# Lower parts of four more weight blocks made by VectorE, and a longer lead for issuing transfers

## The chip, the cores and the metric

The kernel runs on one core of a Trainium2 chip. The metric is the device time of one execution in microseconds (us), taken as the median of several runs. The core's engines are TensorE (PE in the profile, its weight loads PEld), VectorE (DVE), ScalarE (ACT), GpSimd (POOL) and SyncE (SP). Each has its own instruction queue and works through it in order. Transfers are issued from the queues of SP, ACT and POOL.

## What is computed

The reference is a two-layer trunk over 512 tokens of width 1024. Layer A is a conformer convolution module and a squared-ReLU MLP, then one shared set of keys and values is made, and layer B is latent attention and another MLP. The change touches weights of the convolution module (31 taps, a filter per channel):

```python
def conformer_conv(h, w_pw1, b_pw1, w_dw, b_dw, ln_g, ln_b, w_pw2, b_pw2):
    u = h @ w_pw1 + b_pw1
    a, gate = jnp.split(u, 2, axis=-1)
    u = a * jax.nn.sigmoid(gate)
    u = jnp.pad(u, ((0, 0), (CONV_WIDTH - 1, 0), (0, 0)))
    u = lax.conv_general_dilated(u, w_dw[:, None, :], window_strides=(1,), padding='VALID',
                                 dimension_numbers=('NWC', 'WIO', 'NWC'),
                                 feature_group_count=D_MODEL) + b_dw
    u = jax.nn.silu(layer_norm(u, ln_g, ln_b))
    return u @ w_pw2 + b_pw2
```

## The kernel before

**Matrix products.** A product in float32 precision is made of three products in a shorter format: each operand is split into an upper part (rounded) and a lower part (what rounding left), and hi·hi, lo·hi and hi·lo are added in PSUM. A weight block (128 output columns, kept as 128 partitions of 1024 elements) comes into a buffer `raw` by a transfer of 512 KB that SP issues; from it come `wh` (upper) and `wl` (lower). A product of one block is 24 matmuls of 128x512. There are 5 buffers for `raw`, 5 for `wh` and 6 for `wl`, each reused in turn.

**Two ways to the lower part.** They stand in `weight()`, lines 722 to 772. In the first, `split` (line 789), ACT copies `raw` to `wh` in two halves and DVE subtracts, `wl = raw - wh`, in two halves. In the second, for names that `lo_by_dma` (line 88) gives, ACT writes `wl = -raw`, rounded, in two halves, then `wh` in two halves, and POOL issues a transfer that reads the 512 KB of the block from HBM once more and adds them into `wl` (`accum_op`). All 16 blocks of the first pointwise weights (pw1) and of the second (pw2) have such a name, and so have some of the first MLP. Line 754 keeps the first four blocks of pw1 on the first way: `i` counts pw1's blocks in the order of use (columns 0, 8, 1, 9, 2, 10, 3, 11 and so on, a value column and its gate column by turns).

**The convolution module.** When the two products of a channel block are there, DVE multiplies both out of PSUM with the norm's factor (`tmp<-mm,big`), ACT makes the sigmoid (`tmp<-tmp,vt`) and DVE the gated value (`big<-tmp,vt,tmp`). Three of the eight channel blocks (0, 1, 3) are convolved on DVE, 29 instructions `big<-big,vt,big` each, after two by ACT (`big<-big,vt`). The other five (2, 4, 5, 6, 7) go to PE (`taps_tensor`): the gated value is written to DRAM by one transfer on ACT's queue (`dealt<-big`, in `deal_tokens`, line 1151 on), read back in another layout by four more on the same queue (`uu<-dealt`, a quarter of the partitions each), and met by 72 matmuls of 128x128 (`mm<-uu,big`) with band matrices that SP loads (`big<-cw`, nine of 256 KB per channel block). The layer norm follows (`bc<-col,big` sums over channels on PE), then pw2.

**What sets the order.** The kernel does not call the engines directly. `Program` records every operation; `schedule` (line 500 on) places them one after another by costs that it assumes, the most urgent first, where `due` says by when each is needed; `run` repeats this 16 times and issues the operations in the order of the best plan. PE gets filler matmuls (`mm<-ident`) where the plan sees it idle. In `schedule`, line 548 holds a transfer back in the plan until it is at most `LEAD` ahead of its due time. Every instruction is issued on line 640 (`issue`), so that all rows of the profile read L640, and the tiles' names tell them apart. A transfer issued by SP or ACT signals its end on one of eight semaphores (DMAHW0 to DMAHW7 in the order's rows) that the two queues use in turn together; before a semaphore is used again, the transfer eight places earlier must have landed, and the issuing engine waits for that.

Of the kernel before, what the change touches and what calls it, by code (L numbers as in the profile page):

```python
# [87 lines left out]
def lo_by_dma(name):  # L88
    if name[0] == "ff1":
        return name[2] == 0 and name[3] < 4  # L90
    if name[0] == "ff2":
        return name[1] == 0 and name[2] == 3 and name[3] in LAST_BY_DMA
    return name[0] in ("pw1", "pw2")
# [154 lines left out]

PORT = ("tensor_tensor", "scalar_tensor_tensor")

LEAD = 16000.0

BESIDE = 3000.0

# [29 lines left out]
class Program:  # L284
# [166 lines left out]
    def schedule(self, tags):  # L451
# [71 lines left out]
        while left:  # L523
# [19 lines left out]
            while avail[e]:  # L543
# [3 lines left out]
                way = next(w for w in o.ways if w[0] == e)  # L547
                if way[1] == "dma_start" and o.rank > now + LEAD:

                    heappush(future[e], (o.rank - LEAD, o.n, o))  # L550
                    continue
# [92 lines left out]
def trunk(ctx: ExitStack, tc: tile.TileContext, xT, xN, wts, vec, along, rope, cw, out):  # L644
# [72 lines left out]
    def scaled(name, src):  # L717

        lo, hi = ([big(F32R) for _ in range(2)] for _ in range(2))
        for o in range(2):  # L720
            raw = big()
            nc.sync.dma_start(out=raw, in_=src[:, o * T : (o + 1) * T])
            g0 = VEC[GAINS[name[0]]] + 4 * o
            gain = vt[:, g0 : g0 + 4].rearrange("p (k o) -> p k o", o=1).to_broadcast([P, 4, P])
            nc.vector.tensor_tensor(
                out=raw.rearrange("p (k m) -> p k m", m=P), in0=raw.rearrange("p (k m) -> p k m", m=P), in1=gain, op=ALU.mult
            )
            split(raw, slice(0, T), (hi[o], lo[o]))
        return hi, lo

    def weight(key):

        while key not in blocks:
            name, parts = USE[len(blocks)]
            i, n = BLK[parts[0][0]], _cols[BLK[parts[0][0]]]
            if name[0] in GAINS:
                blocks[name] = scaled(name, wts[i])
                continue
            raw, hi, lo = nc.tile(RAW), nc.tile(WH, F32R), nc.tile(WL, F32R)
            step = 256 if i < 2 else n  # L740
            for o in range(0, n, step):
                nc.sync.dma_start(out=raw[:, o : o + step], in_=wts[i, :, o : o + step])
            for other, sign in parts[1:]:
                if sign > 0:
                    nc.gpsimd.dma_start(out=raw, in_=wts[BLK[other]], accum_op=ALU.add)
                else:
                    second = nc.tile(RAW)
                    nc.sync.dma_start(out=second, in_=wts[BLK[other]])
                    for o in range(0, n, 512):
                        nc.vector.tensor_tensor(  # L750
                            out=raw[:, o : o + 512], in0=raw[:, o : o + 512], in1=second[:, o : o + 512], op=ALU.subtract
                        )
            src = raw if len(parts) > 1 else wts[i]
            if i >= 4 and lo_by_dma(name):

                for o in range(0, n, 512):
                    for dst, scale in ((lo, -1.0), (hi, 1.0)):
                        nc.scalar.activation(dst[:, o : o + 512], raw[:, o : o + 512], AF.Copy, scale=scale)
                nc.gpsimd.dma_start(out=lo, in_=src, accum_op=ALU.add)
            else:  # L760
                step = 256 if i < 2 else min(n, 512)
                engines = VG if name[0] in ATT else ("vector",)
                for o in range(0, n, step):
                    split(raw, slice(o, o + step), (hi, lo), engines=engines)
            blocks[name] = hi, lo
        return blocks[key]
# [5 lines left out]
    def products_of(keys, X, t0, n, nk=KT):  # L772

        w = [weight(key) for key in keys]
        pts = [nc.tile(MM) for _ in keys]
        for k in range(nk):
            for (hi, lo), pt in zip(w, pts):
                ks = slice(k * P, (k + 1) * P)
                if isinstance(hi, list):
                    hi, lo, ks = hi[k // 4], lo[k // 4], slice(k % 4 * P, (k % 4 + 1) * P)  # L780

                for j, (a, b) in enumerate(((hi, X[k][0]), (lo, X[k][0]), (hi, X[k][1]))):
                    nc.tensor.matmul(
                        pt[:, :n], lhsT=a[:, ks], rhs=b[:, t0 : t0 + n],
                        start=(k == 0 and j == 0), stop=(k == nk - 1 and j == 2),
                    )
        return pts

    def split(src, s, dst, d=None, engines=("vector",)):

        d = s if d is None else d
        nc.scalar.activation(dst[0][:, d], src[:, s], AF.Copy)
        nc.binary(engines, out=dst[1][:, d], in0=src[:, s], in1=dst[0][:, d].bitcast(F32), op=ALU.subtract)
# [84 lines left out]
    def by_tokens(name, X, first=None):  # L878


        def group(dh, bs, outer):
            pts = {b: nc.tile(MM) for b in bs}
            w = [weight(name + (dh, ku)) for ku in range(4)]
            for ku, b in [(ku, b) for ku in range(4) for b in bs] if not outer else [(ku, b) for b in bs for ku in range(4)]:
                hi, lo = w[ku]

                for n, (j, kk) in enumerate(((0, 0), (1, 0), (0, 1), (1, 1), (2, 0), (2, 1))):
                    k, cs = 2 * ku + kk, slice(kk * DH, (kk + 1) * DH)
                    a, c = ((X[k][0], hi), (X[k][0], lo), (X[k][1], hi))[j]
                    nc.tensor.matmul(  # L890
                        pts[b], lhsT=a[:, b * P : (b + 1) * P], rhs=c[:, cs],
                        start=(ku == 0 and n == 0), stop=(ku == 3 and n == 5),
                    )
                if outer and ku == 3:
                    yield b, dh, pts[b]
            if not outer:
                for b in bs:
                    yield b, dh, pts[b]

        for bs in first or (range(TB),):  # L900
            yield from group(0, bs, False)
        for b in range(TB):
            yield from group(1, (b,), True)
# [57 lines left out]
    def feed_forward(layer, X, F):  # L961
# [6 lines left out]
        for q in range(4):  # L968
# [29 lines left out]
            def sides(q, p):  # L998
                return [weight(("ff2", layer, q, p, u)) for u in range(2)]
# [696 lines left out]
```

## Time and profile before

| | us |
|---|---|
| median of 3 runs (lowest, highest) | 1066.44 (1065.2, 1067.63) |
| the profiled execution, its own time | 1068.46 |
| span of the profiled execution, first to last instruction | 1066.7 |
| PE busy in it | 1045.5 |
| DVE busy | 764.1 |
| ACT busy | 640.9 |
| POOL busy | 141.6 |

The sum of the prediction is made against the profiled execution, which took 1068.46 us, 2.0 us more than the median of the runs and 0.8 us more than the slowest of them. Of its own time 1.8 us lie outside the span. Busy time counts instructions with work; time spent waiting for a semaphore or issuing a transfer isn't in it. PE is busy 98% of the span, so that little can be had by anything but the few stretches in which PE waits or runs slowly.

### The profile page before, as it was taken

The numbers are of one execution on the slowest core, as the hardware profiler recorded it, in microseconds if no ns is written. First come the engines' busy times: TensorE is split into PE (matmuls) and PEld (weight loads), VectorE is DVE, ScalarE is ACT, GpSimd is POOL, SyncE is SP. The second block draws the span as 40 slices with busy tenths as digits, with TensorE's granted clock in tenths as the row PEclk, the third lists the DMA queues.
The fourth block names the chain that finished last, engine by engine and source line by source line (L and its number), as shares of the span: only waits on it lengthen the run. The fifth ranks groups of instructions, "written<-read, shape, count | busy, mean of one in ns | idle before, by whom it ended". The sixth has DMA issues, their size and how long they took to land. (4 is left out here: it accounts for less than half of the span.)

```text
span 1066.7 us, 15181 instructions
## 1 busy us (share of the span) xinstructions
PE 1045.5 (98%) x5284; PEld 884.7 (83%) x5284; DVE 764.1 (72%) x1559; ACT 640.9 (60%) x1343; POOL 141.6 (13%) x165
## 2 busy tenths in 40 slices
PE   8989999999999999999999999999999999999996
PEld 7878988988888888888888888889888888888885
DVE  6497994857438737959988987547574495497698
ACT  8543497766545446545767877558565554454652
POOL 1110011100100100001104533301010010000010
PEclk9989999999999999999999999999999999999998
DMA  9995888657866848658923132557599388485684
GB/s 288 300 254 171 287 211 236 156 168 207 253 171 190 257 126 241 189 182 227 237 69 93 56 100 81 174 182 179 161 245 253 112 235 257 143 243 168 187 237 129
DMA packets 67613, 204.08 MB, mean 191 GB/s; under 512 B 7632, under 2 KB 13904, under 8 KB 67536
## 3 DMA queue, kind: packets, MB, share of 16 engines
q1 hardware_dynamic: 49680, 150.15, 40.9%
q0 software_dynamic: 13536, 49.29, 25.6%
q10 hardware_dynamic: 4320, 3.68, 1.1%
q8 instruction: 41, 0.67, 0.3%
q14 instruction: 36, 0.29, 0.1%
HBM read 197.58 MB, written 5.51 MB: 190 GB/s over the span
## 5 line engine op out<-in xcount | busy, mean ns | idle before, releaser
L640 PE MATMUL mm<-big,wh 128*128 128x512 f32 (+1 forms) x1512 | 441.1, 374 | 1.2 <-ACT wh L640 1.2
L640 PE MATMUL mm<-wh,big 128*128 128x512 f32 (+1 forms) x1216 | 374.7, 387 | 0.0
L640 ACT ACTIVATE wh<-raw 128x512 fp32r<-128x512 f32 (+2 forms) x444 | 251.0, 612 | 117.7 <-PE mm L640 73.8
L640 PEld LDWEIGHTS mm<-big,wh 128*128 128x128 f32 x1512 | 275.6, 188 | 52.4 <-ACT wh L640 1.5
L640 DVE TENSOR_TENSOR wl<-raw,wh 128x512 fp32r<-128x512 f32 (+1 forms) x356 | 227.7, 680 | 106.5 <-ACT wh L640 104.1
L640 PE MATMUL mm<-big,wl 128*128 128x512 f32 (+1 forms) x756 | 282.5, 374 | 0.0
L640 PEld LDWEIGHTS mm<-wh,big 128*128 128x128 f32 x1216 | 226.3, 188 | 46.9
L640 PE MATMUL mm<-wl,big 128*128 128x512 f32 (+1 forms) x608 | 234.9, 387 | 0.1
L640 PEld LDWEIGHTS mm<-big,wl 128*128 128x128 f32 x756 | 142.6, 189 | 25.7 <-DVE wl L640 0.5
L640 PEld LDWEIGHTS mm<-wl,big 128*128 128x128 f32 x608 | 114.2, 188 | 23.4 <-DVE wl L640 0.2
L640 POOL DMA_DIRECT2D raw<-wts x64 | 55.5, 867 | 572.7 <-DMA raw<-wts 190.4
L640 ACT ACTIVATE big<-tmp 128x256 f32<-128x256 f32 (+1 forms) x208 | 95.9, 493 | 43.2 <-DVE tmp L640 37.3
L640 DVE TENSOR_TENSOR big<-big,big 128x512 f32<-128x512 f32 (+4 forms) x103 | 69.8, 698 | 55.9 <-ACT big L640 55.6
L640 ACT ACTIVATE tmp<-mm 128x512 f32<-128x512 f32 (+1 forms) x75 | 41.7, 556 | 103.1 <-PE mm L640 102.0
L640 PE MATMUL mm<-big,big 128*128 128x256 f32 (+3 forms) x520 | 83.5, 310 | 1.8 <-DVE big L640 1.8
L640 PEld LDWEIGHTS mm<-big,big 128*128 128x128 f32 x520 | 73.1, 189 | 7.0 <-DVE big L640 2.3
L640 ACT ACTIVATE big<-mm 128x512 f32<-128x512 f32 (+5 forms) x106 | 56.6, 537 | 33.9 <-PE mm L640 32.9
L640 DVE TENSOR_TENSOR big<-tmp,big 128x512 fp32r<-128x512 f32 (+1 forms) x96 | 60.9, 642 | 15.3 <-ACT big L640 12.7
L640 DVE SCALAR_TENSOR_TENSOR big<-big,vt,big 128x512 fp32r<-128x512 f32 (+29 forms) x95 | 63.3, 736 | 8.0 <-ACT big L640 8.0
L640 DVE TENSOR_TENSOR big<-big,mm 128x512 f32<-128x512 f32 x96 | 63.7, 683 | 3.2 <-PE mm L640 2.8
L640 DVE TENSOR_TENSOR tmp<-big,big 128x512 f32<-128x512 f32 x80 | 53.3, 686 | 8.9 <-ACT big L640 8.9
L640 POOL DMA_DIRECT2D wl<-wts x30 | 26.1, 869 | 213.0 <-ACT wl L640 113.3
(90 smaller groups left out, 775.9 us busy)
## 6 DMA issues: line engine op xcount, KB each, us to landing
raw<-wts SPq DMA_DIRECT2D x222, 512.0 KB, 5.0
raw<-wts POOLq DMA_DIRECT2D x64, 512.0 KB, 7.9
wl<-wts POOLq DMA_DIRECT2D x30, 512.0 KB, 8.4
big<-cw SPq DMA_DIRECT2D x45, 256.0 KB, 5.6
big<-wts SPq DMA_DIRECT2D x12, 256.0 KB, 4.3
row<-along SPq DMA_DIRECT2D x5, 512.0 KB, 5.5
raw<-wts SPq DMA_DIRECT2D x12, 192.0 KB, 2.7
big<-xT SPq DMA_DIRECT2D x8, 256.0 KB, 4.2
```

The lines of the kernel that those rows point to most:

```text
L640: return f(*args, **kwargs)
```

## The change

```diff
-LEAD = 16000.0
+LEAD = 20000.0
...
-            if i >= 4 and lo_by_dma(name):
+            if i >= 8 and lo_by_dma(name):
```

The second edit moves blocks 4 to 7 of pw1 (columns 2, 10, 3 and 11) from the second way to the first: for each, two ACT instructions (`wl = -raw`) and one accumulating transfer of 512 KB on POOL's queue go, and two DVE subtractions come. The first edit lets the plan issue a transfer up to 20 us ahead of its due time where it was 16 us. Since the plan is made anew, the order of the engines' queues shifts in many places. In counts ACT has 8 instructions less, DVE 8 subtractions more, POOL 4 transfers less (its rows fall from 170 to 166), PE has the same number of matmuls, and SP's queue has the same transfers in nearly the same order.

The first place is ACT's queue around the first channel block that is convolved on PE (block 2). The two rows `dealt` and `uu` are its transfers, `tmp_505` (before) and `tmp_521` (now) its sigmoid; `raw_484` and `raw_457` are block 10 of pw1, `raw_544` and `raw_516` block 11. Before:

```order
L640 ACTIVATE tmp_505<-tmp_495,vt_94 128x512 [waits DVE_49]
L640 ACTIVATE big_118<-big_486,vt_94 128x511
L640 ACTIVATE big_520<-big_508,vt_94 128x512 [waits DVE_49]
L640 DMA dealt_529<-big_518 128x512 [waits DMAHW0_49,DVE_49]
L640 ACTIVATE wl_532<-raw_484 128x512 [waits DMAHW2_49,DMASW0_49]
L640 ACTIVATE wl_532<-raw_484 128x512
L640 ACTIVATE wh_547<-raw_484 128x512 [waits PE_49]
L640 ACTIVATE wh_547<-raw_484 128x512
L640 ACTIVATE big_122<-big_508,vt_94 128x511
L640 ACTIVATE wl_586<-raw_544 128x512 [waits DMAHW6_49,DMASW1_49]
L640 ACTIVATE wl_586<-raw_544 128x512
L640 ACTIVATE wh_598<-raw_544 128x512 [waits PE_49]
```

and with the change:

```order
L640 ACTIVATE wl_493<-raw_457 128x512 [waits DMAHW2_49]
L640 ACTIVATE wl_493<-raw_457 128x512
L640 ACTIVATE wh_508<-raw_457 128x512 [waits PE_49]
L640 ACTIVATE wh_508<-raw_457 128x512
L640 ACTIVATE tmp_521<-tmp_503,vt_94 128x512 [waits DVE_49]
L640 ACTIVATE big_527<-big_484,vt_94 128x512
L640 ACTIVATE big_122<-big_484,vt_94 128x511
L640 DMA dealt_545<-big_536 128x512 [waits DMAHW2_49,DVE_49]
L640 ACTIVATE wl_581<-raw_516 128x512 [waits DMAHW6_49]
L640 ACTIVATE wl_581<-raw_516 128x512
L640 ACTIVATE wh_591<-raw_516 128x512 [waits PE_49]
L640 ACTIVATE wh_591<-raw_516 128x512
```

The four instructions of block 10 stood behind `dealt` and now stand ahead of the sigmoid and of `dealt`; block 11's stay between `dealt` and the first `uu`, which is the next row in both. On PE the first block of 72 matmuls that reads `uu_109` stands at the same place, behind the tenth product of pw1.

The second place is DVE's queue before the first value leaves PSUM (`tmp<-mm,big`), where the subtractions of blocks 4 to 7 come in (`stat` is the norm's factor). Before:

```order
L640 TENSOR_TENSOR stat_338<-stat_338 128x4 [waits DVE_49]
L640 SCALAR_TENSOR_TENSOR stat_338<-stat_338 128x4 [waits DVE_49] x2
L640 TENSOR_TENSOR tmp_388<-mm_149,big_381 128x512 [waits Activation_49]
L640 TENSOR_TENSOR tmp_393<-mm_174,big_381 128x512
L640 TENSOR_TENSOR tmp_413<-mm_365,big_381 128x512 [waits PE_49]
L640 TENSOR_TENSOR tmp_477<-mm_295,big_381 128x512
```

and with the change, the last of them:

```order
L640 TENSOR_TENSOR wl_364<-raw_279,wh_324 128x512 [waits DMAHW5_49,Activation_49]
L640 SCALAR_TENSOR_TENSOR stat_345<-stat_345 128x4 [waits DVE_49]
L640 TENSOR_TENSOR wl_364<-raw_279,wh_324 128x512 [waits Activation_49]
L640 TENSOR_TENSOR stat_345<-stat_345 128x4 [waits DVE_49]
L640 SCALAR_TENSOR_TENSOR stat_345<-stat_345 128x4 [waits DVE_49] x2
L640 TENSOR_TENSOR wl_383<-raw_336,wh_374 128x512 [waits DMAHW7_49,Activation_49]
L640 TENSOR_TENSOR wl_383<-raw_336,wh_374 128x512 [waits Activation_49]
L640 TENSOR_TENSOR tmp_397<-mm_149,big_392 128x512 [waits Activation_49]
```

Eight subtractions now stand ahead of the first `tmp<-mm,big`; none of those that follow it is for pw1's first eight blocks.

The third place is PE's queue at the last of the five convolved channel blocks (`uu_124`), behind the block of `uu_109`. Before:

```order
L640 MATMUL mm_1260<-uu_109,big_1100 128x128 x4
L640 MATMUL mm_1260<-uu_109,big_1110 128x128 x4
L640 MATMUL mm_1324<-ident_105 128x128
L640 MATMUL mm_1324<-uu_124,big_1124 128x128 x4
L640 MATMUL mm_1324<-uu_124,big_1135 128x128 x4
```

and with the change:

```order
L640 MATMUL mm_1270<-uu_109,big_1070 128x128 x4
L640 MATMUL mm_1270<-uu_109,big_1077 128x128 x4
L640 MATMUL mm_1347<-ident_105 128x128 x4
L640 MATMUL mm_1347<-uu_124,big_1098 128x128 x4
L640 MATMUL mm_1347<-uu_124,big_1110 128x128 x4
```

One filler `mm<-ident` stood here before, and four stand here now; three that stood at another tile have moved to this one.

## Rows read from the trace of the kernel before

**Rows 1.** The page, busy time of each engine: us (share of span) x instructions.

```profile
PE 1045.5 (98%) x5284; PEld 884.7 (83%) x5284; DVE 764.1 (72%) x1559; ACT 640.9 (60%) x1343; POOL 141.6 (13%) x165
```

**Rows 2.** What PE waited for in the whole span: total us, times, longest us.

```profile
PE mm L640 <- DMA uu<-dealt: 3.7, 1, 3.7
```

**Rows 3.** Timeline of PE at 63 us: start, duration, instruction, [idle before <- releaser].

```profile
63.22 0.39 PE L640 MATMUL mm<-big,wh 128*128 128x512 f32 x1
67.30 11.04 PE L640 MATMUL mm<-uu,big 128*128 128x128 f32 x72 [3.69 <-DMA uu<-dealt]
```

**Rows 4.** Stretches: from:to, length, busy us (instructions) per engine, granted PE clock, DMA share.

```profile
13.00:40.00 27.00, 27.00 (x128) 22.47 (x127) 13.09 (x28) 20.71 (x39) 5.33 (x6) 1.00 1.03 280
...
63.60:67.30 3.70, 0.01 (x2) 0.04 (x1) 3.70 (x7) 3.70 (x8) 0.95 (x2) 0.86 0.76 231
...
107.80:144.30 36.50, 36.50 (x310) 35.73 (x309) 35.62 (x68) 22.27 (x51) 2.59 (x3) 1.00 0.86 250
...
540.00:680.00 140.00, 136.50 (x868) 121.84 (x867) 117.29 (x335) 104.77 (x239) 53.66 (x49) 1.00 0.26 81
```

**Rows 5.** The same view, the matmuls on `uu` alone: first and last channel block.

```profile
67.30:78.40 11.10, 11.03 (x72) 10.84 (x72) 0.00 (x0) 0.74 1.00 225
...
136.00:144.40 8.40, 8.23 (x73) 8.10 (x72) 0.00 (x0) 1.00 0.98 177
```

**Rows 6.** Timeline of ACT from 49 to 62 us.

```profile
49.18 0.33 ACTq L640 DMA_DIRECT2D dealt<-big  x1
49.61 1.16 ACT L640 ACTIVATE wl<-raw 128x512 fp32r<-128x512 f32 x2 [4.58 <-DVE big L640]
...
55.99 6.52 ACTq L640 DMA_DIRECT2D uu<-dealt  x4
```

**Rows 7.** Timeline of DVE from 41 to 55 us.

```profile
41.83 1.29 DVE L640 TENSOR_TENSOR tmp<-mm,big 128x512 f32<-128x512 f32 x2 [2.66 <-PE mm L640]
43.04 1.71 DVE L640 SCALAR_TENSOR_TENSOR big<-tmp,vt,tmp 128x512 f32<-128x512 f32 x2
...
52.46 2.72 DVE L640 SCALAR_TENSOR_TENSOR big<-big,vt,big 128x509 f32<-128x509 f32 x4 [2.49 <-ACT big L640]
```

**Rows 8.** Transfers from 0 to 70 us: queues (packets, MB, share of 16 engines), issues (median us).

```profile
q0 software_dynamic: 1200, 4.39, 33.8%
...
big<-cw SPq DMA_DIRECT2D x18, 256.0 KB, 11.6
...
dealt<-big ACTq DMA_DIRECT2D x1, 256.0 KB, 6.8
uu<-dealt ACTq DMA_DIRECT2D x4, 64.0 KB, 7.6
```

**Rows 9.** Tile `raw`, its one transfer issued at 26.40 us (block 10).

```profile
DMA to landing us min/median/max: 14.3/14.3/14.3
```

**Rows 10.** Tile `raw`, its one transfer issued at 28.40 us (block 11).

```profile
DMA to landing us min/median/max: 19.4/19.4/19.4
```

**Rows 11.** Tile `wl`, 0 to 70 us: duration in ns min/median/max, first and last start.

```profile
L640 ACT ACTIVATE wl<-raw x22: 613/618/635, 16.0 to 68.4; 128x512 fp32r<-128x512 f32 x22
L640 DVE TENSOR_TENSOR wl<-raw,wh x12: 417/420/693, 5.2 to 20.3; 128x256 fp32r<-128x256 f32 x8, 128x512 fp32r<-128x512 f32 x4
```

**Rows 12.** What SP's queue waited for from 0 to 70 us.

```profile
SPq L640 <- DMA big<-cw: 14.0, 7, 7.9
SPq L640 <- DMA raw<-wts: 11.9, 6, 3.5
```

**Rows 13.** Timeline of ACT, transfers for the last convolved channel block.

```profile
129.90 2.21 ACTq L640 DMA_DIRECT2D uu<-dealt  x4
```

**Rows 14.** Timeline of PE at the last convolved channel block.

```profile
135.86 0.39 PE L640 MATMUL mm<-ident 128*128 128x128 f32 x2
136.09 8.20 PE L640 MATMUL mm<-uu,big 128*128 128x128 f32 x72
```

**Rows 15.** Transfers issued from 122 to 132.5 us: the reads of `dealt`.

```profile
uu<-dealt ACTq DMA_DIRECT2D x4, 64.0 KB, 2.7
```

## Prediction

> **What bounds the kernel now.** I read the busy times first: PE is busy 1045.5 of 1066.7 us [rows 1], so the reader is to look for the few places in which it stands or runs slowly. The list of PE's waits has one that counts, 3.7 us in one piece, for a transfer `uu<-dealt` [rows 2]. The timeline puts it behind the tenth product of pw1: the last matmul ends at 63.22 + 0.39 = 63.6 us, and the first block of 72 tap matmuls starts at 67.30 and takes 11.04 us [rows 3]. The same 72 matmuls take 8.20 us in the last channel block [rows 14]. The view by stretches says why: PE stands from 63.6 to 67.3 [rows 4], and in the block behind it the granted clock is 0.74, against 1.00 in the last block [rows 5], so that part of it ran at 1.2 GHz where the rest of the kernel runs at 2.4. The wait thus costs its own 3.69 us and 11.04 - 8.20 = 2.84 us behind it, 6.5 us in all.
>
> Then I followed that wait back. ACT issued the write `dealt` at 49.18 us and the first read `uu` at 55.99, when the write had landed, and the reads were there at 67.30 [rows 6, 3]: one hop of 6.8 us and one of 11.3 us, 18.1 us in all, for 256 KB each. Yet its input was done early: DVE had both gated values at 43.04 + 1.71 = 44.75 us [rows 7]. ACT then stood 4.58 us [rows 6] (that row ascribes it to DVE, which had long been done; the order says what else `dealt` waits for, DMAHW0, so an earlier transfer had to land). The transfer engines are full there: their share is 1.03 from 13 to 40 us [rows 4], a load of band matrices took a median 11.6 us to land, 256 KB like `dealt` [rows 8], and SP stood 14.0 and 11.9 us for transfers in the first 70 us [rows 12]. **So PE waits for transfers that start late and travel slowly among bulk.**
>
> **The change, part by part.**
>
> *Four accumulating transfers go.* From 0 to 70 us POOL's queue moved 4.39 MB in 33.8% of 70 us = 23.7 us of all 16 engines [rows 8]. One of 0.524 MB is 2.8 us, four are 11.3 us of full transfer time, before about 40 us, where the share is 1.03. That is the amount by which other traffic can come forward.
>
> *ACT loses eight instructions* of 0.618 us, 4.9 us [rows 11]; *DVE gains eight subtractions* of at most 0.693 us, 5.5 us [rows 11]. They fall between 13 and 40 us, where DVE is busy 13.09 of 27 us [rows 4]: 18.6 with them, so I cost them at nothing. If that cover were gone, the first `tmp<-mm` would be up to 5.5 us late, and it waited 2.66 us for PE at 41.83 [rows 7]. PE gets these four lower parts sooner than by a transfer.
>
> *The write `dealt` starts earlier.* With the change ACT does block 10's four instructions first, then the sigmoid, then two that begin the taps of a channel block on DVE, then `dealt`, and the ring wait of `dealt` is now on DMAHW2, the transfer that block 10's first instruction waits for too; it adds nothing. Block 10 landed at 26.40 + 14.3 = 40.7 us [rows 9]. Its upper part needs a free buffer, that is the product that ended at 41.83 [rows 7]. From there: two halves 1.2 us, the sigmoid about 0.6 (as another ACT instruction of that shape) [rows 11], the gated value 1.71 / 2 = 0.9 [rows 7], so 44.6; ACT's two others (1.2 us from 43.7) end at 44.9. I put `dealt` at 45.0 us, 4.2 us earlier. With the hops of before, unshortened, the reads land at 45.0 + 18.1 = 63.1 us, just ahead of 63.6. Block 11, whose four instructions still stand between `dealt` and `uu`, landed at 28.40 + 19.4 = 47.8 us [rows 10], before the write would. With relieved transfers the hops shorten too: in the last channel block, the reads land in 2.7 us [rows 15] where they take 7.6 here [rows 8]. So I take the whole wait as gone: **-3.69 us, and with it the slow clock, -2.84 us**. The bounds are 0 and -6.5; I take the end, since both the start and the hops move the right way and either alone is nearly enough.
>
> *The longer lead.* It lets the plan place loads earlier on SP's queue. That queue already stands for buffers and landings [rows 12], and its transfers keep nearly the same order, so I cost it at nothing; what it can do wrong is in the rivals.
>
> *The last channel block.* Three more fillers stand ahead of it: 0.39 us for two [rows 14], so +0.6. Its reads are issued over 2.21 us from 129.90 [rows 13] and PE starts at 136.09 [rows 14]; they now stand behind more of ACT's work. Bounds: 0, if fillers only fill a wait, and +2.2, if the issues come later by their own length. I take +0.6, the fillers' own price, which stands in the order.
>
> *The rest.* The order of layer B's attention shifts a little. PE idles 3.5 of 140 us from 540 to 680 [rows 4]; this could vanish or double, so 0 with bounds of -3.5 and +3.5.
>
> **Sum:** -3.69 - 2.84 + 0.6 = -5.9 us. The profiled execution took 1068.46 us, which becomes 1062.5; it stood 2.0 us above the median, and the same difference takes the median from 1066.44 to **1060.5 us**.
>
> **The rivals.**
>
> *B: DVE sets the end of the convolution, and half the gain is given back.* From 107.8 to 144.3 us DVE is busy 35.62 of 36.5 us [rows 4]: three channel blocks of taps run there without a hole, and the layer norm needs them. PE would arrive earlier and wait at the last channel block or at the sums over channels. What DVE itself gains is its wait of 2.49 us for ACT at 52.46 [rows 7], which goes if ACT no longer stands before `dealt`. Then the time is 1066.44 - 2.5 = 1063.9 us. Against it: PE's filler at 135.86 [rows 14] shows it at most barely waiting there now, and other DVE waits for PE move with PE.
>
> *C: the wait stays.* SP's queue, let loose 4 us earlier by the longer lead, takes up the 11.3 us of transfer time at once, loads of band matrices above all, the ring of eight semaphores is as full as before, and `dealt` and `uu` travel as slowly. Then `dealt` issues near 49.2 us again and the time is 1066.4 us. For it: SP's waits of 14.0 and 11.9 us [rows 12] show loads in store. Against it: the ring's slot for `dealt` is now an early one. The Trainium skill bears on this rival (DMA: Bandwidth & Descriptors, "Queues, rings and completion order"): each transfer engine takes the queues that have work in turn, a packet from each. By it a shorter POOL queue would not shorten a hop while SP's and POOL's later transfers still have work, which is the slow half of C; the 2.7 against 7.6 us of the reads [rows 15, 8] shows that the company matters all the same.
>
> *D: slower.* ACT now holds `dealt` behind block 10. If that block lands late, everything behind it is late, `dealt` first. The point from which it decides: with hops of 18.1 us, `dealt` must issue by 49.2 us to be no later than before, so block 10 must land by 49.2 - 0.9 - 0.6 - 4 x 0.62 = 45.2 us, 18.8 us after an issue at 26.40. It took 14.3 [rows 9], but block 11, two us later, took 19.4 [rows 10]. With 19.4, `dealt` issues at 49.8; with a first hop of 11.6, as the median load of that size [rows 8], and a second of 7.6 to 11.3, the reads land at 69.0 to 72.7, 1.7 to 5.4 us later than before, +3.6 in the middle: 1070.0 us. Against it: the four transfers that go were issued ahead of block 10's landing, and shared the engines with it.
>
> **How the numbers follow.** A measurement of this kernel tells about 0.2% from no change, 2.1 us: faster is below 1064.3, slower above 1068.6. The forecast has 0.68; its own range is 1060.5 with -3.5 (attention) and a little more at the low end, 1056.5, and +1.6 (last block at its bound) and +2 (half of attention's bound) at the high end, 1064.1. B has 0.15, spread over 1063 to 1065, so that two thirds of it count as faster; C has 0.10 and D 0.07. Faster: 0.67 + 0.10 = 0.77; same: 0.01 + 0.05 + 0.09 = 0.15; slower: 0.07 + 0.01 = 0.08. The range takes in the forecast and B, 1056.5 to 1065.2, and leaves out C and D, 0.17.
>
> **What the new profile would show.** Right: no wait for `uu<-dealt` over 0.5 us among PE's waits, `dealt` issued near 45 us, the first 72 tap matmuls in 8.2 us at a granted clock of 1.00, `bc<-col` sums some 5 us earlier. B: PE's waits name DVE near 140 us or `uu` at the last block. C: `dealt` near 49 us and 11 us for the first 72. D: ACT stands for `raw` ahead of the sigmoid, and PE starts the taps after 67.3. I am wrong outright if PE gets a new wait on `wl` from DVE before 40 us, or if the attention stretch moves by more than 3.5 us.

## The result, and the profile after

| | us |
|---|---|
| before, median of 7 runs (lowest, highest) | 1065.20 (1063.87, 1067.63) |
| with the change, median of 7 runs (lowest, highest) | 1069.09 (1068.69, 1070.20) |
| ratio, with its 95% interval | 1.0038 (1.0026 to 1.0050) |
| forecast | 1060.5 (1056.5 to 1065.2) |

The kernel became slower by 0.38%, about 4 us, where 6 us less were forecast. The wait that the prediction set out to remove is gone all the same. The list of PE's waits with the change (total us, times, longest us):

```profile
PE mm L640 <- DVE big L640: 3.6, 6, 1.3
PE bc L640 <- DVE big L640: 1.7, 4, 0.8
PE mm L640 <- POOL big L640: 1.6, 1, 1.6
PE mm L640 <- ACT wh L640: 1.1, 1, 1.1
PE mm L640 <- DVE wl L640: 1.1, 3, 0.5
PE mm L640 <- ACT big L640: 0.9, 2, 0.7
```

The line `uu<-dealt` of [rows 2] isn't there. What is left are short waits, of 1.6 us at most, for DVE above all. At 64 us the timeline of PE reads, with the change:

```profile
64.23 0.39 PE L640 MATMUL mm<-big,wh 128*128 128x512 f32 x1
64.46 8.20 PE L640 MATMUL mm<-uu,big 128*128 128x128 f32 x72
```

PE goes from the tenth product into the 72 tap matmuls without a break, and these take 8.20 us where [rows 3] had 11.04. ACT's queue before it:

```profile
42.77 1.16 ACT L640 ACTIVATE wh<-raw 128x512 fp32r<-128x512 f32 x2
43.83 0.71 ACT L640 ACTIVATE tmp<-tmp,vt 128x512 f32<-128x512 f32 x1
...
46.13 0.34 ACTq L640 DMA_DIRECT2D dealt<-big  x1
...
52.73 3.12 ACTq L640 DMA_DIRECT2D uu<-dealt  x4
```

`dealt` is issued at 46.13 us (49.18 in [rows 6]), behind block 10 and the sigmoid as foreseen, and the four reads are issued by 55.85, some 6.7 us earlier than before: 3.05 us from the earlier start of `dealt`, and 3.4 us because the four issues take 3.12 us for 6.52. The transfers in the first 70 us (queue: packets, MB, share; then median us to landing), beside [rows 8]:

```profile
q0 software_dynamic: 1008, 3.67, 28.9%
...
big<-cw SPq DMA_DIRECT2D x21, 256.0 KB, 7.8
...
dealt<-big ACTq DMA_DIRECT2D x1, 256.0 KB, 6.6
uu<-dealt ACTq DMA_DIRECT2D x4, 64.0 KB, 6.1
```

And three stretches, beside [rows 4]:

```profile
13.00:40.00 27.00, 27.00 (x127) 22.43 (x126) 17.56 (x37) 16.08 (x31) 1.88 (x2) 1.00 0.94 298
107.80:144.30 36.50, 36.42 (x293) 34.68 (x292) 33.15 (x82) 29.61 (x65) 4.31 (x5) 1.00 0.99 295
540.00:680.00 140.00, 134.66 (x839) 118.91 (x839) 115.29 (x321) 103.91 (x237) 55.33 (x49) 1.00 0.28 89
```

DVE's eight subtractions found room (17.56 of 27 us busy). PE no longer stands in the convolution. But from 540 to 680 us PE is busy 134.66 us where it was 136.50.

**Where the gain went** is read from three instructions that every version has: the first `mm<-ident,stat` (behind the layer norm), and the first `bc<-ident,h` behind 500 us and behind 700 us, that is ahead of the attention and behind it. Their rows before and after, from the timelines of PE:

```profile
151.01 0.71 PE L640 MATMUL mm<-ident,stat 128*128 128x128 f32 x4
...
518.31 0.41 PE L640 MATMUL bc<-ident,h 128*128 128x128 f32 x2
...
716.57 0.38 PE L640 MATMUL bc<-ident,h 128*128 128x128 f32 x2
```

```profile
144.32 0.71 PE L640 MATMUL mm<-ident,stat 128*128 128x128 f32 x4
...
513.45 0.41 PE L640 MATMUL bc<-ident,h 128*128 128x128 f32 x2
...
715.46 0.38 PE L640 MATMUL bc<-ident,h 128*128 128x128 f32 x2
```

The front, up to the layer norm, is 6.7 us shorter (144.32 against 151.01). From there to 513 us the change loses 1.8 us, in the attention 3.75 us (202.01 against 198.26), and behind it 1.7 us, to the span's ends of 1067.3 and 1066.7. Of the 3.75 us some 2.8 are waits: PE stands 3.5 us in the attention before, 6.3 us with the change. The same four stretches for every profile, each the difference of two such starts, the last up to the end of the span:

| kernel | front | to the attention | attention | behind it | median of runs, and of before beside it |
|---|---|---|---|---|---|
| before (the profile of the prediction) | 151.01 | 367.30 | 198.26 | 350.1 | |
| before, again (e4) | 149.62 | 367.31 | 198.27 | 350.1 | 1065.01 / 1064.93 |
| the change | 144.32 | 369.13 | 202.01 | 351.8 | 1069.09 / 1065.20 |
| the change, again (e13) | 144.39 | 368.68 | 203.36 | 351.8 | 1070.54 / 1065.33 |
| plan of before held (e1) | 145.48 | 367.10 | 198.17 | 350.2 | 1063.86 / 1064.93 |
| the same, again (e12) | 145.01 | 367.15 | 198.31 | 350.4 | 1064.81 / 1065.22 |
| first edit alone, lead 16 us (e2) | 146.57 | 367.18 | 198.64 | 351.3 | 1066.37 / 1064.93 |
| second edit alone (e3) | 147.86 | 368.12 | 199.48 | 350.9 | 1068.57 / 1064.93 |
| lead 20 us early, 16 late (e5) | 145.02 | 368.30 | 199.62 | 350.6 | 1065.06 / 1064.51 |
| lead 16 us early, 20 late (e6) | 148.29 | 366.90 | 203.24 | 350.8 | 1071.34 / 1064.51 |
| lead 16.1 us (e8) | 147.19 | 366.75 | 199.47 | 349.7 | 1065.68 / 1064.51 |
| lead 12 us (e9) | 146.36 | 368.58 | 203.69 | 352.0 | 1074.03 / 1065.22 |
| lead 20.1 us (e10) | 144.44 | 367.95 | 199.55 | 352.9 | 1066.94 / 1065.22 |
| lead 24 us (e11) | 154.93 | 369.45 | 199.75 | 351.0 | 1076.06 / 1065.22 |
| the change, 3 subtractions off POOL (e7) | 144.17 | 369.02 | 200.33 | 355.9 | 1067.33 / 1064.51 |
| the same, again (e14) | 143.79 | 368.75 | 200.36 | 352.6 | 1067.26 / 1065.33 |
| held plan, 2 subtractions off POOL (e15) | 147.17 | 366.98 | 197.60 | 350.2 | 1064.21 / 1065.33 |

Four profiles with one plan behind the front (before twice, e1, e12) agree in the attention within 0.14 us. The two of the change have one plan as well, and differ there by 1.35 us. The second of them ran at half clock for a time, the first did not (the change, then e13; the third number from the right is the granted clock):

```profile
585.00:595.00 10.00, 9.04 (x53) 7.73 (x53) 9.66 (x33) 5.75 (x16) 4.55 (x5) 1.00 0.28 88
```

```profile
585.00:595.00 10.00, 9.37 (x48) 8.54 (x49) 8.78 (x28) 5.41 (x14) 4.10 (x5) 0.83 0.27 84
```

No other profile of the table has such a stretch in the attention, so that a difference of a microsecond between the others belongs to the plan there. The fronts of e6, e8, e9, e11 and e15 have one before 150 us, and carry it.

### The profile page after: what moved, and what is told of

It is laid out like the page before. It is cut to its first block, busy times and chain, and to the rows that moved or that the text cites. A ratio compares the mean times of both kernels' runs of the same rounds, so it can differ in the third digit from the quotient of the medians.

```text
span 1067.3 us, 15165 instructions
## 1 busy us (share of the span) xinstructions
PE 1047.1 (98%) x5284; PEld 882.4 (83%) x5284; DVE 770.8 (72%) x1567; ACT 636.7 (60%) x1335; POOL 138.9 (13%) x161
## 4 chain that ended last, share of the span: by engine, by line
PE 79%; DVE 11%; ACT 4%; DMA 4%; issue 1%; SPq 0%; DVEq 0%; ACTq 0%
PE mm L640 77%; DVE big L640 6%; DMA raw<-wts 3%; DVE wl L640 2%; PE bc L640 2%; ACT big L640 2%; DVE stat L640 2%; ACT wh L640 1%; ACT junk L640 1%; DVE h L640 1%; ACT wl L640 0%; DVE tmp L640 0%; DMA vt<-vec 0%; SPq L640 0%; DVE raw L640 0%
## 5 line engine op out<-in xcount | busy, mean ns | idle before, releaser
L640 DVE TENSOR_TENSOR wl<-raw,wh 128x512 fp32r<-128x512 f32 (+1 forms) x362 | 233.2, 681 | 166.3 <-ACT wh L640 161.3
L640 POOL DMA_DIRECT2D wl<-wts x26 | 23.0, 883 | 205.1 <-ACT wl L640 111.8
```

The lines of the kernel that those rows point to most:

```text
L640: return f(*args, **kwargs)
```

## The experiments

Three theories stood at the start. One: the front gains about 6.5 us, and the plan, made anew for the whole kernel, lost it in later stages. Two: the longer lead costs. Three: the profile of before caught a rare wait, so that there was little to gain.

**e1 and e12: the edit without a new plan.** The plan is made as before, and at the time of issuing the four accumulating transfers and the eight `wl = -raw` are dropped and DVE's subtraction follows each half of `wh`:

```diff
+            swap = getattr(op, "late_lo", ())
+            if swap is None:
+                continue
             self.issue(
...
+            if swap:
+                l, r, w = swap
+                self.nc.vector.tensor_tensor(out=real(l), in0=real(r), in1=real(w.bitcast(F32)), op=ALU.subtract)
```

> Blocks 4 to 7 get their lower parts from DVE, but the plan of before (made with accumulating transfers and a lead of 16 us) is kept for every other instruction, so that nothing behind the convolution moves. Theory 1 (the front gains about 6.5 us, and the re-made order of the later stages gave it back): no wait for uu of more than 1 us at 63 us, the 72 matmuls behind it in 8.2 us, attention stretch as in the kernel before, time 4 to 7 us below the kernel before. Theory 2 (the longer lead is what costs): the same result, since the lead is 16 us here. Theory 3 (the profile of before shows a rare wait, and most runs have little of it): within 2 us of the kernel before.

Measured: 1063.86 us against 1064.93, ratio 0.9995 (0.9985 to 1.0005). The tap matmuls, from its timeline of PE:

```profile
65.27 8.20 PE L646 MATMUL mm<-uu,big 128*128 128x128 f32 x72
```

No wait, 8.20 us, and nothing lost behind the front: its profiled execution took 1062.69 us, 5.8 us less than that of before. (It was also the lowest of its 11 runs, as that of before was a high one.) ACT's queue in it:

```profile
46.60 0.33 ACTq L646 DMA_DIRECT2D dealt<-big  x1
...
49.20 0.84 ACTq L646 DMA_DIRECT2D uu<-dealt  x2
...
56.85 0.31 ACTq L646 DMA_DIRECT2D uu<-dealt  x1
```

The order is that of before, with `dealt` ahead of block 10, and yet `dealt` goes 2.6 us earlier, without the 4.58 us for which ACT stood there [rows 6]. It landed in 2.4 us, where it took 6.8 [rows 8]; the share of the transfer engines was 0.47 meanwhile. So taking out the four transfers was enough here, and block 10's place in ACT's queue was not needed. In the median of runs, though, the gain is 1.1 us and not clear of nothing. The same kernel once more:

> The kernel with the plan of before and DVE's subtractions for blocks 4 to 7 once more, to narrow what the front is worth in the median of runs. Prediction's size: 4 to 7 us below the kernel before. What the first such run gave: 0 to 2 us below it.

Measured: 1064.81 us against 1065.22, ratio 0.9994 (0.9985 to 1.0003). Its profile has no wait either (the 72 matmuls start at 64.41 us and take 8.20), and its profiled execution, 1062.64 us, is again the lowest of its runs. In these two executions the mechanism is right. In the median of runs the gains are 1.1 and 0.4 us, neither clear of nothing, and far from 6.5. What the slower runs of this kernel have, no profile shows.

**e4: the kernel before once more.** No edit.

> The kernel before once more, for the granted clock of each of its runs and a second profile. Theories 1 and 2: the wait of 3 to 4 us for uu and the slow 72 matmuls are in this profile too, and the mean granted clock is 0.993 in its runs. Theory 3: the second profile has a wait under 2 us, and runs near 1064 us show a mean clock of 0.996 or more.

Measured: 1065.01 us (11 runs from 1063.09 to 1067.51); the profiled execution took 1067.10. From its timelines of ACT and PE:

```profile
56.43 4.48 ACTq L640 DMA_DIRECT2D uu<-dealt  x4
...
66.32 9.90 PE L640 MATMUL mm<-uu,big 128*128 128x128 f32 x72 [2.40 <-DVE big L640]
```

The last read is issued by 60.91 us, and PE stands 2.40 us (the row names DVE, but the reads landed 5.6 to 8.1 us after their issue, the last one so near 66.2) and runs the block in 9.90: 4.1 us in all, where the first profile had 6.5. So the wait's size changes from run to run; at 2.40 us it is above the 2 us that theory three had set. The runs of before beside the experiments lie between 1062.23 and 1069.54 us, and the execution from which the prediction took its 6.5 us, 1068.46, is near their slow end. The granted clock, which is on record for each run as the mean of the whole, agrees. It was 0.993 in that execution. Of the 30 runs of before beside e1 to e4, 18 had 0.997 or 0.998, and no profile of the table with a stretch at half clock has more than 0.996. So, by this sign, most runs of before have no such stretch, and the 2.84 us of slow clock aren't in them. With a median of 1065.0, 1.8 us outside the span and the later stretches of the table (367.3, 198.3, 350.1), the median's front ends near 147.5 us: this estimate, which takes the scatter to lie in the front, as it does between the two profiles of before (1.39 us in the front for 1.36 us in all), leaves some 3 us to what the changed kernel reaches, 144.4. Theory three holds for the size.

**e2 and e3: each edit alone,** with `i >= 8` and a lead of 16 us, or `i >= 4` and 20 us.

> Only the first edit: i >= 8, lead of 16 us, plan made anew. Theory 1: the early gain is there, and the attention stretch lies somewhere between 4 us better and 6 us worse than before, by what the new plan happened to be. Theory 2: 4 to 7 us faster than before, with no PE waits in the attention stretch that before lacks. Theory 3: within 2 us of before, plus or minus the plan.

> Only the second edit: lead of 20 us, all twelve later blocks of pw1 by accumulating transfers, plan made anew. Theory 1: the wait for uu stays or moves with the plan, attention again as the plan has it. Theory 2: slower than before by 4 to 8 us, and the waits of the attention stretch (1.5 us at 550 us) are there. Theory 3: like theory 1.

Measured: 1066.37 us, ratio 1.0010 (1.0000 to 1.0020), and 1068.57 us, ratio 1.0037 (1.0022 to 1.0051). Neither gains; e3 loses as much as the whole change, and keeps a wait at 66 us, which the first edit removes. That spoke for theory two.

**e5, e6, e8 to e11: is it the lead?** First the lead by part of the plan, with `i >= 8`:

```diff
-                if way[1] == "dma_start" and o.rank > now + LEAD:
-                    heappush(future[e], (o.rank - LEAD, o.n, o))
+                lead = LEAD if now < 150e3 else 16000.0
+                if way[1] == "dma_start" and o.rank > now + lead:
+                    heappush(future[e], (o.rank - lead, o.n, o))
```

(e6 has `now >= 150e3`), and `LEAD = 16100.0`, a step too small to matter for any transfer. In these expectations theory L is theory two, and theory P says that every new plan is a draw, whatever the lead.

> First edit, and a lead of 20 us only in the first 150 us of the plan, 16 us after. Theory L (a longer lead costs in the later stages, by loads that come in earlier): 2 to 3 us faster than with the whole change, near 1066. Theory P (any new plan shuffles the attention stretch, and the time there is a draw of some 5 us): anything from 1063 to 1070, with the attention stretch (work of PE from 520 to 680 us) losing 0 to 6 us against the kernel before, and not by what the lead is there.

> First edit, and a lead of 20 us only after the first 150 us of the plan, 16 us before. Theory L: as slow as the whole change, 1068 to 1070. Theory P: again anything from 1063 to 1070.

> First edit and a lead of 16.1 us, a change of the lead that is too small to matter for any transfer, but makes another plan. Theory L: within 1 us of the first edit alone with 16 us (1066.4). Theory P: it can lie 2 us or more from it, up or down, and what differs is the attention stretch.

Measured: 1065.06, 1071.34 and 1065.68 us. A lead of 20 us in the later stages had now been slow three times of three, as theory two has it, and 16.1 us lies within 0.7 us of 16. (1071.34 us is above the range of either theory.) Then other leads, throughout:

> First edit and a lead of 12 us throughout. Theory L (the longer the lead, the more splits of weights that are not yet due are pulled into the attention stretch, where DVE and ACT have no room): at or below the first edit with 16 us, 1064 to 1066.5. Theory P (each plan is a draw, and the lead only chooses the draw): as likely 1068 to 1071 as 1064 to 1067.

> First edit and a lead of 20.1 us, too small a step to matter for any transfer, another plan. Theory L: 1067.5 to 1071.5 like the three runs with 20 us in the later stages (1069.1, 1068.6, 1071.3). Theory P: as likely 1064 to 1067 as above.

> First edit and a lead of 24 us. Theory L: 1069 or more. Theory P: as likely 1064 to 1067 as above.

Measured: 1074.03, 1066.94 and 1076.06 us. The shorter lead is slow, slower than either theory had it, and 20.1 us is 2 to 3.6 us faster than 20 us (1069.09 and 1070.54). So theory two falls: a lead of 20 us is not slow as such, though 24 us is slow too. Each lead makes another plan, and the plans lie between 1065 and 1076 us. In the attention, whose computing neither edit changes (the lead holds for its transfers too), the nine new plans take 198.6 to 203.7 us, all more than the plan of before. With 24 us it was the front, too, by the very wait that the change was to remove, at another channel block (PE's waits):

```profile
PE mm L640 <- DMA uu<-dealt: 8.4, 1, 8.4
```

**e7, e13, e14, e15: what a bad plan does in the attention.** In the changed kernel PE waits 1.34 us for DVE, up to 552.15 us. These rows of DVE and of POOL stand ahead of it, and the last is PE's:

```profile
547.34 1.18 DVE L640 TENSOR_SCALAR stat<-stat 128x2 f32<-128x2 f32 x2
...
549.03 1.18 DVE L640 TENSOR_TENSOR stat<-stat 128x2 f32<-128x2 f32 x2
550.24 1.05 DVE L640 SCALAR_TENSOR_TENSOR stat<-stat 128x2 f32<-128x2 f32 x2
...
547.47 2.52 POOL L640 TENSOR_TENSOR wl<-raw,wh 128x384 fp32r<-128x384 f32 x2 [31.76 <-ACT wh L640]
550.26 1.01 POOL L640 TENSOR_TENSOR wl<-raw,wh 128x384 fp32r<-128x384 f32 x1 [0.27 <-ACT wh L640]
...
552.15 1.70 PE L640 MATMUL mm<-big,big 128*128 128x256 f32 x12 [1.34 <-DVE big L640]
```

The `stat` instructions have two elements a partition, and one takes some 0.16 us elsewhere. Here three pairs take over 1 us each, just where POOL subtracts. In e7 the plan is kept, and the first three of POOL's subtractions are issued to DVE:

```diff
+            if engine == "gpsimd" and method == "tensor_tensor" and moved < 3:
+                engine, moved = "vector", moved + 1
```

> The whole change with its plan kept; only the first three subtractions wl<-raw,wh that the plan gave to POOL (128x384, at 547 to 551 us) are issued to DVE at the same place in the order. Theory P with a mechanism: DVE's tiny stat instructions stood about 1 us each behind POOL's subtractions in that stretch (1.18, 1.18 and 1.05 us for pairs that take 0.35 elsewhere), and PE waited 1.34 us for the result; without POOL's work beside them they take under 0.5 us a pair, that wait falls below 0.6 us, and the time falls by 0.5 to 1.5 us. If POOL's work is not what holds them: they stay at 1 us, and the time stays within 0.3 us or rises by the 1.4 us that DVE does more.

Measured: 1067.33 us, ratio 1.0020 (1.0007 to 1.0032), with runs from 1065.30 to 1071.13; the profiled one is the slowest. PE's wait of 1.34 us is gone from it. With that spread, both kernels once more, on one chip:

> The changed kernel once more, on the chip of e14: 3 to 5 us above the kernel before.

> The changed kernel's plan with three subtractions moved from POOL to DVE, once more, beside e13. If POOL's hold on DVE is a real part of the loss: 1 to 2 us below e13. If the first result was the scatter of runs: within 0.5 us of e13.

Measured: 1070.54 and 1067.26 us, 3.3 us apart where 1 to 2 were expected, their ratios to before 1.0047 (1.0030 to 1.0063) and 1.0026 (1.0012 to 1.0040). The `stat` instructions from 535 to 560 us, in ns min/median/max, of e13 and then of e14:

```profile
L640 DVE SCALAR_TENSOR_TENSOR stat<-stat x13: 150/154/854, 535.7 to 551.7; 128x2 f32<-128x2 f32 x13
L640 DVE TENSOR_TENSOR stat<-stat x10: 150/160/980, 534.9 to 550.9; 128x2 f32<-128x2 f32 x10
...
L640 DVE TENSOR_SCALAR stat<-stat x3: 169/169/982, 543.1 to 547.1; 128x2 int32<-128x2 int32 x2, 128x2 f32<-128x2 f32 x1
```

```profile
L643 DVE SCALAR_TENSOR_TENSOR stat<-stat x13: 149/154/161, 535.2 to 549.9; 128x2 f32<-128x2 f32 x13
L643 DVE TENSOR_TENSOR stat<-stat x8: 150/160/161, 536.1 to 548.6; 128x2 f32<-128x2 f32 x8
...
L643 DVE TENSOR_SCALAR stat<-stat x3: 160/168/169, 542.6 to 547.1; 128x2 int32<-128x2 int32 x2, 128x2 f32<-128x2 f32 x1
```

The longest falls from 982 to 169 ns, PE's wait at 551 us is gone, and the attention is 3.0 us shorter. But e13 is the profile with the stretch at half clock, which by the two profiles of the change accounts for 1.35 us of the 3.0. Between the first profile of the change and that of e7, neither of which has one there, the same edit took 1.7 us off the attention (202.01 to 200.33). So the three subtractions on POOL are 1.7 of the 3.75 us that the change lost there; as they take 0.55 us each on DVE for 1.0 and more on POOL, that is the price of both, their own length and the hold. The medians carry the clock as well: four of e13's six runs have a granted clock of 0.996 or less, two of e14's twelve. It is no rule by count: the plan of before has 11 `stat` instructions of over 0.4 us in the attention, the change 7, and before is the faster one. What would count is whether PE waits behind them; that is argued, not tried. The same in the held plan, for its first two (`moved < 2`):

> The plan of before, blocks 4 to 7 by DVE, and the first two of POOL's subtractions (those beside the stat chain at 546 us) issued to DVE. If POOL holds DVE there: the stat instruction of 0.93 us takes 0.2, PE's wait of 0.69 us for stat falls by 0.5 or more, and the time is 0.3 to 0.8 us below the held kernel (about 1 to 2 us below before). If not: equal to the held kernel.

Measured: 1064.21 us against 1065.33, ratio 0.9984 (0.9972 to 0.9996). Its waits and `stat` instructions:

```profile
PE bc L649 <- DVE stat L649: 0.5, 1, 0.5
...
L649 DVE TENSOR_SCALAR stat<-stat x4: 163/169/170, 535.8 to 548.8; 128x2 int32<-128x2 int32 x3, 128x2 f32<-128x2 f32 x1
```

The 934 ns of the held kernel became 170, and the attention 197.60 us, the shortest of all. Of PE's waits for `stat`, 1.2 us in two in the held kernel, 0.5 us in one are left, at 26 us. This is the one version clear of before, by 0.16%, and barely so, as the best of many; from the held kernel's own runs, 1063.86 and 1064.81, it can't be told apart, so that the expected 0.3 to 0.8 us stay undecided. Its profile would be better still but for the layer norm, where PE ran at half its clock for a time after a wait (granted clock of the stretch):

```profile
138.00:148.00 10.00, 8.72 (x58) 8.10 (x57) 7.95 (x34) 8.05 (x18) 1.73 (x2) 0.83 0.79 202
```

## Why the prediction was wrong

**The wait for `uu`: right in mechanism, too large.** "I take the whole wait as gone: -3.69 us, and with it the slow clock, -2.84 us" happened, by the steps named: `dealt` at 46.13 us (45.0 foreseen), no wait, 8.20 us at a granted clock of 1.00. The term was mis-sized: it came from one execution near the slow end, and "the same difference takes the median" carried the whole of it into the median run. By the estimate at e4 the new plan gains some 3 us in the front of the median run; with everything else held, the edit gained 1.1 and 0.4 us in the medians, neither clear of nothing.

**"the hops shorten too"** happened by little with the change: `dealt` took 6.6 us for 6.8, a read a median of 6.1 for 7.6. The earlier start did half of the work, and the quicker issue of the four reads, which the sum did not name, the other half. That the write's hop hardly changed agrees with the rule that was set beside rival C (the Trainium skill, DMA: Bandwidth & Descriptors, "Queues, rings and completion order"), by which the queues that have work take turns. While `dealt` was under way, the transfer engines' share was still 1.03. In the held kernel's two profiles it was 0.47 and 0.35, and the write landed in 2.4 and 2.0 us. So the hop goes by what else moves just then, and one profile doesn't tell it.

**DVE's subtractions and ACT's relief at nothing**: right, DVE 17.56 of 27 us for the 18.6 foreseen (in the held kernel PE waited 0.51 us for `stat` at 26 us). **The last channel block, +0.6**: right in size; the fillers took 1.06 us for 0.39, and there was no wait behind them.

**"The rest", "0 with bounds of -3.5 and +3.5", is the step that failed,** and with it the longer lead's "so I cost it at nothing". The attention lost 3.75 and 5.1 us in two profiles, the stretch ahead of it 1.8 and 1.4, that behind it 1.7 twice: 7.3 us, and 8.1 with the stretch at half clock, where the term had 0. With the plan held nothing was lost there (e1 and e12 in the table). The bound was drawn from the idle time of PE in the old plan, as if the new plan were the old one with small shifts. It is another plan, drawn from a spread that the experiments show as 11 us wide, and the plan of before was a good draw. That is what the 4 us are: some 3 us gained in front, by estimate, and 7.3 lost behind.

**The rivals.** B, C and D named places in the convolution. None happened; the loss came from stages whose computing the edits don't change. "I am wrong outright if [...] the attention stretch moves by more than 3.5 us" was the right alarm, but slower had a chance of 0.08, and nearly all of that was D's.

**What stays open.** Of the 3.75 us in the attention, the 2 that are left without the three subtractions were not tried apart. Of the losses outside it, the 1.7 us behind show in part as waits for lower parts of weights (0.53 us at 890 us). In e7's profile that stretch was 4 us longer, in e14's, the same kernel, 0.8: most of the difference is scatter, with PE at a granted clock of 0.83 from 885 to 895 us in e7. Neither these losses nor the 1.4 to 1.8 us ahead of the attention were tried apart.

## What to carry to other kernels

Where a planner orders the kernel, an edit is two changes: what it does, and a new plan everywhere. Price them apart, by holding the old plan and patching the issue, and take the spread of plans from a parameter moved by a hair (16 to 16.1, 20 to 20.1) before crediting or blaming an edit. Size a wait from several executions: the one profiled may be among the slowest.

## What the runs showed of the hardware

A DVE instruction of two elements a partition, 0.16 us alone, took up to 0.98 us beside POOL's subtractions of 1.0 us and more, and ended with them (the last pair at 551.29 us, POOL at 551.27). With the subtractions on DVE, at 0.55 us, all took 0.15 to 0.17 us again. The Trainium skill has this (SBUF — State Buffer, "SBUF: two separate sides"): the port pair that the two engines share is held for a whole instruction, and the other one waits; it names DVE instructions in a two-port mode or with two SBUF inputs. The trace agrees in size: the delay is that of a POOL instruction, not of the data that DVE moves. Which of the two kinds each `stat` instruction is, no run here shows.
